# A diffusion mixer layer with two kinds of heads: the recurrence stage's PE work put in the order of the text

## The chip, the core and the metric

The kernel runs on one core of a Trainium2 chip. The metric is the device time of one execution in microseconds, the median of several runs. A profiled execution gives the trace; its span is the time from its first to its last instruction.

The engines are TensorE (PE, with its weight loads as PEld), VectorE (DVE), ScalarE (ACT), GpSimd (POOL) and SyncE (SP), which issues most DMAs.

## The reference

One layer on 1024 latent and 256 context tokens of width 1024, all in float32: a modulated RMSNorm, one input projection, a differential-attention group (8 heads), a bidirectional RWKV-7 recurrence (16 heads of 64 in two directions), an output projection over both, a gated residual and a final RMSNorm.

```python
h = rmsnorm(x, norm_g) * (1 + scale) + shift
q, k, v, g_a, u_b, g_b = split(h @ w_in)
# attention, per head: two score maps, their softmaxes p
a = p[:, :, 0] - lam * p[:, :, 1]
o_a = rmsnorm(einsum('bhqk,bkhv->bqhv', a, v), subln_g) * (1 - lam_init) * silu(g_a)
# recurrence, per head and direction (reversed for d = 1)
def step(S, (r_t, w_t, k_t, v_t, kk_t, b_t)):
    sa = einsum('bhvk,bhk->bhv', S, -kk_t)
    S = S * w_t + sa * b_t + v_t * k_t
    return S, einsum('bhvk,bhk->bhv', S, r_t)
y = y_forward + y_backward
o_b = (groupnorm(y) * lnx_g + lnx_b + bonus) * silu(g_b)
out = rmsnorm(x + gate * (concat(o_a, o_b) @ w_out), final_g)
```

Latent tokens also attend to 512 cached context tokens, and their scans start from a cached state; the layer returns the keys, the values and the final states of the context too.

## The kernel before

**Stages.** Up to 1243 us the kernel projects the tokens and writes the operands of the recurrence to scratch in DRAM. Then `mix_phase` runs the recurrence, and beside it the attention and most of the output projection. What is left of these and the final norm is the tail, from 2392 us on.

**The recurrence in chunks.** A scan is cut into chunks of 32 tokens, so that a step handles a whole chunk by matrix products. A step handles four pairs of heads (`NL`), both heads of a pair and both directions. The four pairs are two *duos* `w`, each with a bank of PSUM, `bank[w]`. There are 80 steps: two groups of pairs, five segments of 256 tokens (the context and four latent ones), eight chunks each. Two steps (`HN`) form a *part* `j`, whose operands lie in the slot `slots[w, j % 2]`: `L` (the weights) and `R` (the moving side, with the state in rows 0 to 63, the values in 64 to 95, and sa in 96 to 127). The two slots of a duo take turns.

**One step**, `step(j, k, fill)`, is in the text:
1. the *sa* group, L894: 8 products of 96 rows for each bank, each f32 product being two instructions in the profile; ACT copies the result to `R[96:128]` (L899, four copies for each bank);
2. `fill(0)`, a portion of attention and other background work;
3. the *st* group, L908, 8 products for each bank; DVE multiplies the result by the decay into the state of the next step (L917, two operations for each bank);
4. `fill(1)`, a second portion;
5. the *y* group, L931, 8 products for each bank, into another part of the same bank; ACT copies it to `ys` (L933).

sa and st are put ahead by `high_priority(offset=500)` (`HPC`), y isn't (`HPY = 0`). The order on each engine isn't that of the text: a scheduler sets it, by priorities and by its estimate of when operands are ready, so it may cut a group in two and put attention between.

**Slots.** At the first step of part j, `load_part(j + 1)` fills the other slot, last read by the y groups of part j − 1. For each duo these are one load of `kt` into `L` (L772), two of `ra` into `L` (L775) and four of `vb` into `R` (L781); `load_inv` adds one of a chunk's inverse, `Tb`, for each duo (L792, three buffers, `TBUF`). Ahead of the second step of part j, `prep(j + 1, w)` multiplies `Tb` with rows of `L` for each duo (L802, all into one bank `yb`) and ACT copies that back to `L` (L805). SP issues these loads in its own order, and each waits there for the slot.

**Attention** is a generator. For a block n of 128 queries of a head: `scores(n, m, c)` (L1047) makes one 512-key chunk of map m, DVE takes it out of PSUM with a maximum (L1050) and ACT the exponential (L1058); `combine` (L1078, DVE) subtracts the second map; `trans` (L1086) turns a chunk on PE in four products and ACT copies it to `aT` (L1088); `values` (L1101) multiplies four pieces of it with the values. Each yield tells a cost, and `fill` takes as many pieces as its credit allows; the credit grows in each step by the whole cost over the number of steps, times `RATE`, 0.86. `turn` also advances `outs` (the norm of attention's result; `ob` at L1138 on POOL), `norms` (the norm of y, which reads `y` from DRAM into `yn`) and `projs`.

**Projection.** `project(j)` does a quarter of the output projection (the rows of two attention heads and two pairs) for ten token tiles, each of eight products in three forms (L1286 to L1288, into PSUM `pso`), and adds to `acc` in DRAM (L1280). The fourth quarter is done in the tail by `final`, which also applies the gate (L1357) and adds the residual (L1358, both on POOL).

## Time and profile before

| what | us |
|---|---|
| runs: 2642.70, 2634.27, 2647.06; median | 2642.7 |
| the profiled execution | 2639.98 |
| its span | 2637.7 |
| projection, to | 1243 |
| recurrence, 80 steps, to | 2392 |
| tail, to | 2638 |

The busy share of each engine, the causes of PE's waits and the granted clock stand in the prediction, with the rows themselves. In a row of instructions stand the line, the engine and the operation, then what is written and what is read, how many, and busy time and mean ns of one. The part behind the second bar is the time for which the engine stood idle just before these instructions, and whose end it was that ended it. In a row of the timeline stand the start, the time until the end of the last of the instructions put together, and what they are. The column PEclk is the clock granted to TensorE as a share of full speed.

The DMA queues, as the page has them, move these transfers of the recurrence:

```profile
L<-kt SPq DMA_DIRECT2D x80, 512.0 KB
L<-ra SPq DMA_DIRECT2D x160, 128.0 KB
R<-vb SPq DMA_DIRECT2D x320, 32.0 KB
y<-ys SPq DMA_DIRECT2D x160, 64.0 KB
yn<-y SPq DMA_DIRECT2D x20, 512.0 KB
```

### The profile page before, as it was taken

The numbers are of one execution on the slowest core, as the hardware profiler recorded it, in microseconds if no ns is written. First come the engines' busy times: TensorE is split into PE (matmuls) and PEld (weight loads), VectorE is DVE, ScalarE is ACT, GpSimd is POOL, SyncE is SP. The second block draws the span as 40 slices with busy tenths as digits, with TensorE's granted clock in tenths as the row PEclk, the third lists the DMA queues.
The fourth block names the chain that finished last, engine by engine and source line by source line (L and its number), as shares of the span: only waits on it lengthen the run. The fifth ranks groups of instructions, "written<-read, shape, count | busy, mean of one in ns | idle before, by whom it ended". The sixth has DMA issues, their size and how long they took to land. (4 is left out here: it accounts for less than half of the span.)

```text
span 2637.7 us, 61554 instructions
## 1 busy us (share of the span) xinstructions
PE 2361.2 (90%) x23907; PEld 1908.8 (72%) x23907; DVE 1475.6 (56%) x2960; ACT 1274.8 (48%) x2928; POOL 1199.6 (45%) x1735
## 2 busy tenths in 40 slices
PE   6999999999999999998688888888889898898886
PEld 4788888888888888786466766666666676676664
DVE  5656565555455655434457556664455455566466
ACT  3334443333333433322476666766556357674243
POOL 4234344243433443375365525747467542125386
PEclk9999999999999999998798889889989999999997
DMA  7465656565645565567878777878867887676534
GB/s 237 111 165 131 177 147 176 135 169 161 160 129 155 136 176 131 167 158 185 176 155 187 162 160 145 184 164 191 211 155 194 203 198 171 141 171 220 176 104 161
DMA packets 532418, 437.63 MB, mean 166 GB/s; under 512 B 161991, under 2 KB 466291, under 8 KB 532128
## 3 DMA queue, kind: packets, MB, share of 16 engines
q1 hardware_dynamic: 530032, 427.96, 64.9%
q0 software_dynamic: 2096, 5.75, 1.1%
q8 instruction: 188, 3.08, 0.5%
q14 instruction: 102, 0.84, 0.1%
HBM read 258.69 MB, written 163.86 MB: 160 GB/s over the span
## 5 line engine op out<-in xcount | busy, mean ns | idle before, releaser
L1047 PE MATMUL sc<-ka,q 128*128 128x512 f32 (+1 forms) x832 | 296.7, 457 | 20.2 <-DVE pb L1050 12.3
L1050 DVE TENSOR_SCALAR_CACHE_REDUCE pb<-sc,mn 128x512 f32<-128x512 f32 x256 | 191.7, 749 | 135.1 <-PE sc L1047 110.4
L1101 PE MATMUL po<-vk,aT 128*128 128x128 f32 x1600 | 244.8, 296 | 9.1 <-ACT aT L1088 8.6
L1058 ACT ACTIVATE pb<-pb,mn 128x1536 f32<-128x1536 f32 (+1 forms) x160 | 218.4, 1366 | 60.2 <-DVE pb L1050 58.7
L1101 PEld LDWEIGHTS po<-vk,aT 128*128 128x128 f32 x1600 | 221.3, 205 | 29.4 <-ACT aT L1088 12.2
L479 POOL TENSOR_SCALAR ta<-ta,ka 128x256 f32<-128x256 f32 x80 | 88.1, 1101 | 297.8 <-DVE bk L477 297.7
L734 POOL TENSOR_TENSOR tmp<-aw,tt 128x31 f32<-128x31 f32 (+15 forms) x310 | 164.6, 531 | 127.9 <-DMA aw<-kt 54.9
L456 ACT COPY km<-ptk 64x256 f32<-64x256 f32 x320 | 117.4, 367 | 192.1 <-PE ptk L453 165.7
L899 ACT COPY R<-bank 32x128 f32<-32x128 f32 x640 | 163.4, 255 | 68.7 <-PE bank L894 59.4
L917 DVE TENSOR_TENSOR R<-bank,wc 64x256 f32<-64x256 f32 x312 | 131.4, 421 | 113.5 <-PE bank L908 98.4
L736 POOL TENSOR_TENSOR tt<-tt,tmp 128x31 f32<-128x31 f32 (+15 forms) x310 | 182.4, 588 | 18.2
L1047 PEld LDWEIGHTS sc<-ka,q 128*128 128x128 f32 x832 | 145.6, 208 | 55.7 <-DVE pb L1050 21.5
L1078 DVE SCALAR_TENSOR_TENSOR pb<-pb,cc,pb 128x512 f32<-128x512 f32 (+1 forms) x208 | 170.6, 866 | 2.5
L805 ACT COPY L<-yb 32x384 f32<-32x384 f32 x312 | 146.3, 469 | 40.1 <-PE yb L802 35.9
L802 PE MATMUL yb<-L,Tb 32*32 32x96 f32 x2496 | 96.1, 261 | 76.3 <-DMA L<-kt 68.7
L450 DVE TENSOR_TENSOR km<-pg,msk 128x512 f32<-128x512 f32 x80 | 55.1, 689 | 183.5 <-PE pg L449 168.7
L1050 DVE TENSOR_SCALAR_CACHE_REDUCE pb<-sc 128x512 f32<-128x512 f32 (+1 forms) x160 | 101.2, 635 | 91.2 <-PE sc L1047 75.3
L1088 ACT COPY aT<-pa 128x512 f32<-128x512 f32 (+1 forms) x208 | 115.9, 570 | 62.9 <-PE pa L1086 60.5
L1086 PE MATMUL pa<-ident,pb 128*128 128x128 f32 x800 | 133.2, 292 | 14.0 <-ACT acc L1278 7.8
L802 PEld LDWEIGHTS yb<-L,Tb 32*32 32x32 f32 x2496 | 62.6, 111 | 105.9 <-DMA L<-kt 56.3
L908 PEld LDWEIGHTS bank<-R,L 128*64 128x64 f32 x2560 | 99.3, 151 | 54.6 <-ACT R L899 23.7
L908 PE MATMUL bank<-R,L 128*64 128x64 f32 x2560 | 122.9, 243 | 16.7 <-ACT R L899 16.4
(355 smaller groups left out, 6463.2 us busy)
## 6 DMA issues: line engine op xcount, KB each, us to landing
kt<-km SPq DMA_DIRECT2D x160, 256.0 KB
L<-kt SPq DMA_DIRECT2D x80, 512.0 KB
acc<-acc SPq DMA_DIRECT2D x50, 512.0 KB
ra<-ra SPq DMA_DIRECT2D x160, 128.0 KB
L<-ra SPq DMA_DIRECT2D x160, 128.0 KB
R<-vb SPq DMA_DIRECT2D x320, 32.0 KB
y<-ys SPq DMA_DIRECT2D x160, 64.0 KB
yn<-y SPq DMA_DIRECT2D x20, 512.0 KB
```

The lines of the kernel that those rows point to most:

```text
L734: e.tensor_tensor(mv, aw[:n, t, t + 1:CH].unsqueeze(2).broadcast_to([n, w, j]), tt[:n, t:t + 1, 0:j].broadcast_to([n, w, j]), op=ALU.mult)
L736: e.tensor_tensor(tt[:n, t + 1:CH, 0:j], tt[:n, t + 1:CH, 0:j], mv, op=ALU.add)
L802: nc.tensor.matmul(pp[32 * q:32 * q + 32, n:n + 96], Tb[96:128, e, HN * q + c, :], L[96:128, e, q // 2, q % 2, c, 0:96], start=True, stop= ...
L805: nc.scalar.copy(L[96:128, :, q // 2, q % 2, :, 0:96], pp[32 * q:32 * q + 32, 0:192 * HN].rearrange("p (e c y) -> p e c y", e=2, y=96))
L899: nc.scalar.copy(R[96:128, k, e, :, hv(h)], bank[w][u:u + 32, 0:128].rearrange("p (d v) -> p d v", d=2))
L908: nc.tensor.matmul(bank[w][hv(h), o_:o_ + 64], L[:, e, h, d, k, 0:64], R[:, k, e, d, hv(h)], start=True, stop=True, tile_position=(0, 64 * h))
L1047: nc.tensor.matmul(sc, q[:, v, m, qc], ka[:, m, 0:kn], start=(v == 0), stop=(v == 1))
L1050: nc.vector.tensor_scalar(pm[:, c * 512:c * 512 + kn], sc, -0.125, mn[:, c - 1:c] if c else None, op0=ALU.mult, op1=ALU.min, accum_out=mn[ ...
L1058: nc.scalar.activation(v, v, AF.Exp, bias=mn[:, c:c + 1], scale=-1.0, accum_out=B["l3"][:, m, k:k + 1])
L1078: nc.vector.scalar_tensor_tensor(a, B["p"][1][:, v], B["cc"], a, op0=ALU.mult, op1=ALU.add)
L1086: nc.tensor.transpose(pt[:, t * P:(t + 1) * P], B["p"][0][:, 512 * c + t * P:512 * c + (t + 1) * P], ident)
L1101: nc.tensor.matmul(po, B["aT"][c][:, t * P:(t + 1) * P], vk[:, t, :], start=(c == 0 and t == 0), stop=(c == last and t == nt - 1))
```

## The change

1. **PE in the order of the text.** Just ahead of `att = attention()` the kernel enters `tc.manual_schedule(engines={nc.tensor.engine})`. From there to the end PE's instructions stand as the text has them; the scheduler still orders the other engines.
2. **The step in the text.** sa for both banks; the copies to `R[96:128]`, those of the second bank now on DVE; at the second step of a part `prep` of the first duo; `fill(0)`; st for both banks; the state update; y for both banks directly behind it; `prep` of the second duo; `fill(1)`. `R` and the bank hold direction ahead of pair now. The priority stays around the copies and the state update.
3. **Attention's pieces** come in another order: scores of the first map alternate with `values` of the block before the last, scores of the second map with `trans` of the last block, and `combine` is done at the end of its own block. `aT` has three buffers for two; a copy per block (`l3` to `l`) goes. `fill`'s rate is 1.06 in the first half of the steps and 0.68 in the second.
4. **Slots in fewer transfers.** `kt` and `ra` lie in scratch by pairs of pairs, so that a duo's `ra` is one load; `vb` comes in two loads for each duo and `Tb` in one for both duos (one buffer). Nine loads a part take the place of 16, both `kt` first, `Tb` third in the text. `y` is stored in 4 transfers for 8, of runs of 1 KB for 512 bytes, and read back by two loads for one.
5. **Projection.** The quarters of the second group of pairs are started after segment 0 instead of 3, so that two tiles of the third quarter come in the recurrence and not in the tail, and the residual add moves from POOL to DVE. Yields are added: `NDEL` and `ODEL` grow from 6 and 8 to 10 and 14, and `project` and `final` get two more each.

On PE, in the middle of the first part of the recurrence, a step looked as follows before; L894 is the sa group (of `bank1` here), L802 the build, L908 st, L931 y, and the rows with `sc`, `pa` and `po` are scores, `trans` and `values` of attention.

```order
L894 MATMUL bank1_12299<-R11_11594,L11_11593 32x64 x8
L802 MATMUL yb_12300<-L00_11563,Tb0_2_12714 32x96 x9
L908 MATMUL bank0_12298<-R01_11574,L01_11573 64x64 x8
L1047 MATMUL sc0_1_1_1_12496<-ka_0_1_12312,q_0_0_12304 128x512 x2
L802 MATMUL yb_12300<-L00_11563,Tb0_2_12714 32x96 x7
L1086 MATMUL pa0_0_0_12483<-ident_78,pb0_12301 128x128 x4
L1086 MATMUL pa0_0_1_12592<-ident_78,pb0_12301 128x128 x4
L908 MATMUL bank1_12299<-R11_11594,L11_11593 64x64 x8
L1047 MATMUL sc0_1_1_2_12587<-ka_0_2_12315,q_0_0_12304 128x512 x2
L931 MATMUL bank0_12298<-R01_11574,L01_11573 32x64 x8
L1047 MATMUL sc0_2_0_0_12651<-ka_0_0_12309,q_0_0_12304 128x512 x2
L1101 MATMUL po0_0_12603<-vk_0_0_12318,aT0_0_0_12488 128x128 x4
```

And a like step after the change, where L893 is sa, L803 the build, L913 st, L936 y, and L1057, L1089 and L1104 are scores, `trans` and `values`.

```order
L893 MATMUL bank0_12282<-R01_11574,L01_11573 32x64 x8
L893 MATMUL bank1_12283<-R11_11594,L11_11593 32x64 x8
L803 MATMUL yb_12284<-L00_11563,Tb2_12707 32x96 x16
L1057 MATMUL sc0_3_1_1_12902<-ka_0_1_12298,q_0_0_12290 128x512 x2
L1089 MATMUL pa0_2_2_12906<-ident_78,pb0_12287 128x128 x4
L1057 MATMUL sc0_3_1_2_12913<-ka_0_2_12301,q_0_0_12290 128x512 x2
L1104 MATMUL po0_2_12927<-vk_0_0_12304,aT0_2_0_12841 128x128 x4
L1057 MATMUL sc0_4_0_0_12937<-ka_0_0_12295,q_0_1_12324 128x512 x2
L1104 MATMUL po0_2_12927<-vk_0_1_12306,aT0_2_1_12852 128x128 x4
L913 MATMUL bank0_12282<-R01_11574,L01_11573 64x64 x8
L913 MATMUL bank1_12283<-R11_11594,L11_11593 64x64 x8
L936 MATMUL bank0_12282<-R01_11574,L01_11573 32x64 x8
```

Before, the two st groups stood apart, with scores and transposes between, and the y group of `bank0` came two rows behind the second of them, that of `bank1` 18 rows behind (not shown); now both banks of a group stand side by side, and y behind st with nothing between (the row of y of `bank1` is the next). Here the y group waits for DVE's state update, which reads the same bank. From the first row of the recurrence on PE to its last, the kind of work (attention and projection, sa, st, y, build, transposes of the state) changed 1013 times from row to row before, and changes 478 times now. The products of that stretch are nearly the same: 746 scores and 742 now, 700 `trans` and 700 `values` in both, and 160 and 176 of each of the projection's three forms.

On SP's queue, the loads of one part's slots looked as follows before (`L00` and `L10` are `L` of the two duos).

```order
L772 DMA L00_11563<-kt_67 64x2x1024
L775 DMA L00_11563<-ra_66 64x8x64 x2
L781 DMA R00_11564<-vb_68 32x2x128 x4
L772 DMA L10_11583<-kt_67 64x2x1024
L775 DMA L10_11583<-ra_66 64x8x64 x2
L781 DMA R10_11584<-vb_68 32x2x128 x4
L792 DMA Tb1_2_12716<-td0_77 32x2x256
```

And so they look now.

```order
L781 DMA R00_11564<-vb_68 32x2x256
L772 DMA L00_11563<-kt_67 64x2048
L772 DMA L10_11583<-kt_67 64x2048
L793 DMA Tb2_12707<-td0_77 32x4x256
L781 DMA R00_11564<-vb_68 32x2x256
L782 DMA L00_11563<-ra_66 64x16x64
L781 DMA R10_11584<-vb_68 32x2x256 x2
L782 DMA L10_11583<-ra_66 64x16x64
```

The two `kt` loads stood apart by six transfers and now follow each other; `Tb` came last and now stands behind them.

The diff, cut:

```diff
@@ -42,12 +42,12 @@
-RATE = 0.86
+RATES = (1.06, 0.68)
...
-TBUF = 3
+TBUF = 1
...
-NDEL = 6
-ODEL = 8
+NDEL = 10
+ODEL = 14
...
@@ -769,16 +769,18 @@
-            nc.sync.dma_start(L[64:128].rearrange("r e h d c y -> r e (h d c y)"),
-                              s["kt"][p:p + 2, sg + 1, f].rearrange("e r h d y -> r e (h d y)"))
-            for e in range(2):
-                nc.sync.dma_start(L[0:64, e, :, :, :, 64:128].rearrange("r h d c y -> r (h d c) y"),
-                                  s["ra"][p + e, sg + 1, f].rearrange("r h d (c y) -> r (h d c) y", y=HD))
+            nc.sync.dma_start(L[64:128].rearrange("r e h d c y -> r (e h d c y)"),
+                              s["kt"][p // 2, sg + 1, f].rearrange("r e h d y -> r (e h d y)"))
+        load_inv(j)
+        for w in duos:
+            p = p0 + 2 * w
+            L, R = slots[w, j % 2]
...
-                for c in range(HN):
-                    t1 = t0 + CH * (HN - 1 - c if d else c)
-                    nc.sync.dma_start(R[64:96, c, :, d, :], s["vb"][t1:t1 + CH, p * P:(p + 2) * P].rearrange("t (e v) -> t e v", e=2))
+                src = s["vb"][t0:t0 + CH * HN, p * P:(p + 2) * P].rearrange("(c t) y -> t c y", t=CH)
+                nc.sync.dma_start(R[64:96, :, d].rearrange("t c e v -> t c (e v)"), src[:, ::-1] if d else src)
+            nc.sync.dma_start(L[0:64, :, :, :, :, 64:128].rearrange("r e h d c y -> r e (h d c) y"),
+                              s["ra"][p // 2, sg + 1, f].rearrange("r e h d (c y) -> r (e h d c) y", y=HD))
...
@@ -884,53 +884,62 @@
-        with ahead(HPC):
-            for w in duos:
-                L, R = slots[w, j % 2]
-                for d in range(2):
-                    for e in range(2):
-                        for h in range(2):
-                            u = 64 * e + 32 * h
-                            nc.tensor.matmul(bank[w][u:u + 32, 64 * d:64 * d + 64], L[0:96, e, h, d, k, 96:128],
-                                             R[0:96, k, e, d, hv(h)], start=True, stop=True, tile_position=(0, u))
+        for w in duos:
+            L, R = slots[w, j % 2]
+            for d in range(2):
...
-                        nc.scalar.copy(R[96:128, k, e, :, hv(h)], bank[w][u:u + 32, 0:128].rearrange("p (d v) -> p d v", d=2))
-        fill(0)
+                        nc.tensor.matmul(bank[w][u:u + 32, 64 * d:64 * d + 64], L[0:96, e, h, d, k, 96:128],
+                                         R[0:96, k, d, e, hv(h)], start=True, stop=True, tile_position=(0, u))
...
-                L, R = slots[w, j % 2]
+                R = slots[w, j % 2][1]
...
-                    for d in range(2):
-                        for h in range(2):
-                            o_ = 256 + 128 * e + 64 * d
-                            nc.tensor.matmul(bank[w][hv(h), o_:o_ + 64], L[:, e, h, d, k, 0:64],
-                                             R[:, k, e, d, hv(h)], start=True, stop=True, tile_position=(0, 64 * h))
+                    for h in range(2):
+                        u = 64 * e + 32 * h
+                        (nc.vector.tensor_copy if w else nc.scalar.copy)(
+                            R[96:128, k, :, e, hv(h)], bank[w][u:u + 32, 0:128].rearrange("p (d v) -> p d v", d=2))
+        later_prep = k == HN - 1 and j + 1 < n_part
+        if later_prep:
+            prep(j + 1, 0, yb)
+        fill(0)
+        for w in duos:
+            L, R = slots[w, j % 2]
+            for e in range(2):
+                for d in range(2):
+                    for h in range(2):
+                        o_ = 256 + 128 * d + 64 * e
+                        nc.tensor.matmul(bank[w][hv(h), o_:o_ + 64], L[:, e, h, d, k, 0:64],
+                                         R[:, k, d, e, hv(h)], start=True, stop=True, tile_position=(0, 64 * h))
+        with ahead(HPC):
+            for w in duos:
...
-                    dst = R[0:64, k + 1]
+                    dst = slots[w, j % 2][1][0:64, k + 1]
...
-                    nc.vector.tensor_tensor(dst[:, :, :, hv(h)], bank[w][hv(h), 256:512].rearrange("p (e d v) -> p e d v", e=2, d=2),
-                                            wcs[p0][hv(h), 2 * w:2 * w + 2, sg + 1, :, c:c + 1].broadcast_to([HD, 2, 2, HD]), op=ALU.mult)
-        fill(1)
+                    nc.vector.tensor_tensor(dst[:, :, :, hv(h)], bank[w][hv(h), 256:512].rearrange("p (d e v) -> p d e v", e=2, d=2),
+                                            wcs[p0][hv(h), 2 * w:2 * w + 2, sg + 1, :, c:c + 1].rearrange("p e d o -> p d e o").broadcast_to([HD, 2, 2, HD]), op=ALU.mult)
...
-        with ahead(HPY):
-            for w in duos:
-                L, R = slots[w, j % 2]
-                for e in range(2):
-                    o_ = P + 64 * e
-                    for h in range(2):
-                        for d in range(2):
-                            q = 64 * d + 32 * h
-                            nc.tensor.matmul(bank[w][q:q + 32, o_:o_ + 64], L[:, e, h, d, k, 64:96], R[:, k, e, d, hv(h)],
-                                             start=True, stop=True, tile_position=(0, q))
-                nc.scalar.copy(ysb[m, g][:, c % 4, 2 * w:2 * w + 2], bank[w][:, P:2 * P].rearrange("p (e v) -> p e v", e=2))
+        for w in duos:
+            L, R = slots[w, j % 2]
+            for e in range(2):
+                o_ = P + 64 * e
+                for h in range(2):
+                    for d in range(2):
+                        q = 64 * d + 32 * h
+                        nc.tensor.matmul(bank[w][q:q + 32, o_:o_ + 64], L[:, e, h, d, k, 64:96], R[:, k, d, e, hv(h)],
+                                         start=True, stop=True, tile_position=(0, q))
+        for w in duos:
+            nc.scalar.copy(ysb[m, g][:, c % 4, 2 * w:2 * w + 2], bank[w][:, P:2 * P].rearrange("p (e v) -> p e v", e=2))
+        if later_prep:
+            prep(j + 1, 1, yb)
+        fill(1)
...
@@ -1191,25 +1194,37 @@
...
-            if p is not None:
-                weight(p)
-                combine(p, 0)
-            if pp is not None:
-                values(pp, len(st[pp]["ch"]) - 1)
+                if c < nk - 1 and vp:
+                    old_values()
+                    yield 0.87
+            while vp:
+                old_values()
...
-            if p is not None:
-                trans(p, 0)
-                yield 0.43
-            for c in range(nk):
-                if c < kp_ - 1:
-                    combine(p, c + 1)
-                scores(n, 1, c)
-                yield cost
-            for c in range(nk, kp_ - 1):
-                combine(p, c + 1)
+            for c in range(max(nk, kp_)):
+                if c < kp_:
+                    trans(p, c)
+                    yield 0.43
+                if c < nk:
+                    scores(n, 1, c)
+                    yield cost
+            if new:
+                weight(n)
+                for c in range(nk):
+                    combine(n, c)
+            if kp_ > 1:
+                values(p, 0)
+                yield 0.87
...
@@ -1355,7 +1369,7 @@
-                nc.gpsimd.tensor_tensor(x, x, y, op=ALU.add)
+                nc.vector.tensor_tensor(x, x, y, op=ALU.add)
...
@@ -1371,6 +1385,7 @@
+    ctx.enter_context(tc.manual_schedule(engines={nc.tensor.engine}))
...
@@ -1384,14 +1399,13 @@
-    rate = total / (2 * n_tick) * RATE
...
-            state["credit"] += rate / 2
+            state["credit"] += total / (4 * n_tick) * RATES[2 * state["t"] // n_tick]
...
@@ -1422,10 +1436,6 @@
-                load_inv(j + 1)
-        if k == HN - 1 and j + 1 < n_part:
-            for w in duos:
-                prep(j + 1, w, yb)
...
@@ -1436,7 +1446,7 @@
-        if sg == 3:
+        if sg == (3 if m < 5 else 0):
...
```

71 lines of the change are left out of this document (34 added, 37 removed).

## The prediction

> **What bounds the kernel now.** The first view is the busy time by engine.
>
> ```profile
> PE 2361.2 (90%) x23907; PEld 1908.8 (72%) x23907; DVE 1475.6 (56%) x2960; ACT 1274.8 (48%) x2928; POOL 1199.6 (45%) x1735
> ```
>
> PE is the engine nearest to full, and the change alters its order from the recurrence on. The second view cuts the rest of the span at the first recurrence matmul (1243 us), in the middle of the 80 steps (1800) and at their end (2392).
>
> ```profile
> core 0: us, PE busy (x) PEld busy (x) DVE busy (x) ACT busy (x) POOL busy (x), PEclk, DMA share, GB/s
> 1243.00:1800.00 557.00, 463.55 (x6905) 358.62 (x6905) 335.67 (x832) 367.91 (x953) 296.99 (x545) 0.87 0.79 167
> 1800.00:2392.00 592.00, 524.12 (x6747) 400.72 (x6750) 316.74 (x773) 361.83 (x927) 263.37 (x451) 0.93 0.78 184
> 2392.00:2638.00 246.00, 192.24 (x958) 152.09 (x946) 149.28 (x302) 84.01 (x176) 139.17 (x157) 0.89 0.48 163
> ```
>
> In the recurrence PE stands still for 557 − 463.6 + 592 − 524.1 = 161 us of 1149 (14.4 us a step in the mean), and works at 0.87 and 0.93 of its clock. DVE is busy for 0.60 and 0.54 of it, so it isn't the bound there yet. The third view says what ended PE's idle time between 1243 and 2392 us.
>
> ```profile
> engine line waited for: us in total, times, longest us
> PE yb L802 <- DMA L<-kt: 68.7, 31, 10.1
> PE bank L908 <- ACT R L899: 16.4, 16, 3.3
> PE bank L894 <- ACT ys L933: 13.0, 10, 2.7
> PE sc L1047 <- DVE pb L1050: 9.1, 9, 4.1
> PE pso L1286 <- DVE acc L1280: 8.5, 2, 8.2
> PE pa L1086 <- ACT acc L1278: 7.8, 2, 5.9
> PE po L1101 <- ACT aT L1088: 7.8, 8, 3.1
> ```
>
> One wait stands out: L802, which builds the operands of the next two steps, waits 31 times for the kt load of its slot. The next largest is four times smaller. The last lines that matter here are the groups of the instructions that the change moves, in the same stretch: PE first, then DVE.
>
> ```profile
> L802 PE MATMUL yb<-L,Tb 32*32 32x96 f32 x2496 | 96.1, 261 | 76.3 <-DMA L<-kt 68.7 <-ACT pb L1058 2.7 <-ACT L L805 2.3
> L931 PE MATMUL bank<-R,L 128*32 128x64 f32 x2540 | 82.1, 235 | 4.5 <-DVE R L917 4.5
> ```
>
> ```profile
> L917 DVE TENSOR_TENSOR R<-bank,wc 64x256 f32<-64x256 f32 x312 | 131.4, 421 | 113.5 <-PE bank L908 98.4 <-DMA wc<-wc 5.6 <-ACT aT L1088 3.6
> L1078 DVE SCALAR_TENSOR_TENSOR pb<-pb,cc,pb 128x512 f32<-128x512 f32 (+1 forms) x182 | 147.0, 853 | 2.1
> L1050 DVE TENSOR_SCALAR_CACHE_REDUCE pb<-sc,mn 128x512 f32<-128x512 f32 x228 | 170.7, 749 | 125.8 <-PE sc L1047 104.9 <-PE pa L1086 12.9 <-DVE pb L1050 0.5
> ```
>
> The y group L931 waits for the state update L917 for 4.5 us in all 80 steps. That small number is the weight of this case: the change puts the y group directly behind the st group, so that this wait is met in every step.
>
> **Slot loads: −65 us.** The wait as it looks in the timeline:
>
> ```profile
> 1604.37 0.59 SPq L772 DMA_DIRECT2D L<-kt  x1
> 1605.75 0.69 PE L908 MATMUL bank<-R,L 128*64 128x64 f32 x16
> 1606.40 0.74 DVE L1050 TENSOR_SCALAR_CACHE_REDUCE pb<-sc,mn 128x512 f32<-128x512 f32 x1
> 1607.68 0.85 DVE L917 TENSOR_TENSOR R<-bank,wc 64x256 f32<-64x256 f32 x2
> 1610.80 0.85 PE L802 MATMUL yb<-L,Tb 32*32 32x96 f32 x28 [2.51 <-DMA L<-kt]
> 1611.58 0.43 PE L931 MATMUL bank<-R,L 128*32 128x64 f32 x16
> 1612.59 0.59 SPq L772 DMA_DIRECT2D L<-kt  x1
> ```
>
> A slot may be refilled only after the y group of its last step has read it, and y stands at the very end of the step, behind both portions of attention, and slides further as the last choice of the order. The kt load of one duo is issued at 1604.4, and that of the other at 1612.6, right behind the y group of the other bank (1611.58 + 0.43): 8.2 us later. L802 gets the first one 6.4 us after its issue. Afterwards both y groups stand together and ahead of the second portion of attention, both kt loads stand next to each other on SP's queue, and between that y and the build stand half a step, a whole one and the next sa, some 20 us at 14.4 a step, for a load of 6.4; the mean wait was 68.7/31 = 2.2 us, the longest 10.1. I take 65 of the 76.3 us of L802 away and leave 11 for the longest ones. Bounds: −76 and 0 (release not earlier, or the longer transfers land later). PE then waits next for the y group itself, below.
>
> **Fewer changes of kind on PE: −30 us.** Between the first and last recurrence matmul the order of PE changes between kinds of work 1013 times before and 478 times afterwards, 535 fewer. The price of one, from two like transposes:
>
> ```profile
> 1707.22 0.60 PE L1086 MATMUL pa<-ident,pb 128*128 128x128 f32 x4
> 1707.66 1.06 PE L1101 MATMUL po<-vk,aT 128*128 128x128 f32 x8
> 1708.55 0.60 PE L1086 MATMUL pa<-ident,pb 128*128 128x128 f32 x4
> 1709.08 0.69 PE L908 MATMUL bank<-R,L 128*64 128x64 f32 x16
> 1709.69 0.43 PE L931 MATMUL bank<-R,L 128*32 128x64 f32 x16
> 1710.06 0.73 PE L1047 MATMUL sc<-ka,q 128*128 128x512 f32 x2
> ```
>
> Four transposes followed by another full-array product take 0.44 us from start to start, and followed by a recurrence group 0.53: 0.09 us for the way in. The way back shows nothing (y to scores 0.37, less than its 0.43). So 535 × 0.09 = 48 if every change costs it, 24 if only one of two does. I take 30; bounds −10 and −55.
>
> **Waits of st for the copies of R and of sa for ys: −25 us.** Of 16.4 + 13.0 = 29.4 us most goes, since a whole portion of attention now stands between sa and st, and the ys copy has the second portion to run beside. Half of the R copies moves from ACT to DVE (4 a step), which can bring new waits there. Bounds −29 and +20.
>
> **The y group behind the state update: +86 us.** From the rows above: at 1605.75 the st group of a bank takes 0.69, ends at 1606.44, and the update ends at 1608.53, 2.1 us later, since two evictions of L1050 were ahead on DVE. Undisturbed, the update starts about 0.1 us behind its group and both halves take 2 × 0.42. Now all four updates (4 × 0.421 = 1.68) follow two st groups, and the two y groups stand on PE right behind, with nothing between. From the end of bank 0's st group: the updates end at 0.11 + 1.68 = 1.8, y can start its second bank some 0.15 later, and in that time PE has 0.69 (st of bank 1) + 0.43 (y of bank 0) to do: 1.95 − 1.12 = 0.8 us of standing, at least, in each step. At most, one combine (0.853) and one eviction (0.749) are ahead on DVE: 0.8 + 1.6 = 2.4. DVE is busy with other things for about half of the time, with operations of some 0.75 us, so the mean addition is near 0.5 × 0.75 = 0.4 or, since recurrence work goes first, less: I take 0.3, so 1.1 us, nearer to the floor. 78 steps with an update: 78 × 1.1 = 86; bounds 62 and 187. Behind the waiting y rows on PE stand the building of the second duo's operands and the second portion of attention; DVE's evictions and ACT's exponentials starve with them.
>
> **The start of attention: +10 us.**
>
> ```profile
> 1243.70:1258.90 15.20, 9.14 (x208) 6.65 (x208) 3.31 (x9) 8.20 (x26) 6.10 (x11) 0.64 0.86 225
> 1265.17 1.19 PE L1047 MATMUL sc<-ka,q 128*128 128x512 f32 x2 [6.30 <-DMA ka<-klo]
> ```
>
> The first keys land at 1265.2. Before, PE does 9.1 us of recurrence work meanwhile; now the first scores stand in the text behind the first sa group, and everything behind them waits. I take +10; bounds 0 and +20.
>
> **The clock: −10 us.** The windows of 3.4 us around the wait above:
>
> ```profile
> 1606.30:1609.70 3.40, 1.99 (x32) 1.40 (x26) 2.97 (x9) 2.47 (x6) 3.09 (x5) 1.00 0.98 192
> 1609.70:1613.10 3.40, 2.30 (x52) 1.75 (x52) 0.10 (x1) 2.28 (x6) 2.93 (x7) 1.00 0.03 8
> 1613.10:1616.50 3.40, 3.40 (x40) 2.65 (x38) 2.50 (x7) 2.83 (x5) 2.96 (x6) 0.50 0.90 199
> ```
>
> Two windows with PE busy for 1.99 and 2.30 of 3.40 us are followed by one at half clock. At a granted clock of 0.87 and 0.93 the recurrence loses 557 × 0.13 + 592 × 0.07 = 114 us of PE's full-speed time. The long slot waits go, but a stand of about 1.1 us is added to each step, which alone leaves 2.3 of 3.4 us busy, the share of the second row. So I credit 10 of the 114; bounds −100 and +40. The Trainium skill, page "TensorE: Matmul & The Clock Gate", section "Why this matters for your kernels", says it otherwise: only idle gaps of more than about 3 us between bursts bring the clock down. The rows here disagree, as the longest gap in the two windows is the 2.51 us before L802; by that page of the Trainium skill the new short stands would cost no clock, which is the first rival below.
>
> **The tail: −12 us.**
>
> ```profile
> PE pxo L1144 <- POOL ob L1138: 11.2, 3, 9.5
> L1286 PE MATMUL pso<-wohi,ohi 128*128 128x512 f32 x80 | 34.3, 429 | 9.4 <-ACT ohi L1270 5.5 <-DVE acc L1280 2.7 <-DVE bv L996 0.8
> L1358 POOL TENSOR_TENSOR x<-x,y 128x1024 f32<-128x1024 f32 x10 | 24.9, 2487 | 3.3 <-DMA x<-x_sample 2.6 <-DMA x<-x_prompt 0.7
> L1280 DVE TENSOR_TENSOR acc<-pso,acc 128x512 f32<-128x512 f32 x20 | 13.3, 688 | 36.9 <-PE pso L1288 17.7 <-DMA acc<-acc 16.0 <-PE pso L1287 3.1
> ```
>
> Two of ten tiles of a projection move from the tail into the recurrence, 16 × 3 matmuls of 0.43 = 20.6 us of PE, which is no gain by itself where PE is the bound in both. The residual add costs 2.49 us on POOL and by the half-size row of DVE about 2 × 0.69 = 1.4: about 1 us for each of the last two on the end chain. Seven tiles instead of one stand behind the last attention and can cover the 9.5 us wait for POOL's ob: −9.5 − 2, about −12. Against it, the final product's weights are loaded with only about 5 us of PE work beside them. Bounds −30 and +25.
>
> **Everything else at nothing.** In text order a row that isn't ready holds all rows behind it. The four attention and projection waits in the table (9.1 + 8.5 + 7.8 + 7.8 = 33) may go, as attention is spread with more distance, or grow to half a microsecond in each step (+40). I take 0. The rates 1.06 and 0.68 move attention to the first half and remove none of it; the y stores and norm loads run on queues that no PE wait of the table names.
>
> **The sum.** The profiled execution took 2639.98 us, its span 2637.7. −65 − 30 − 25 + 86 + 10 − 10 − 12 = −46: 2640 − 46 = **2594 us**. The median of the runs shown is 2642.7, 2.7 above this execution.
>
> **Rivals.**
> - *The clock stays up.* If the gate wants a longer gap than 1.1 us, the stands cost only themselves, and with the slot waits gone about half of the 114 us comes back instead of 10: −50 more, 2544 us. For it: the longest waits (10.1) are the slots'. Against it: the rows at 1606 and 1609. The section of the Trainium skill named above has this rule.
> - *Even.* The stand of y costs 1.1 + 46/78 = 1.7 us a step and takes everything back: 2640.
> - *Slower: y behind a full DVE.* From 1.7 us a step on, the kernel gets slower. DVE gets 4 copies of R a step (half of L917's 0.42 for half as many elements a row, an estimate: 0.8 us of 14.4) and, by the rates, 1.06/0.86 = 1.23 of the attention in the first half, where attention is about two thirds of its work: 335.7/557 = 0.60 busy becomes 0.60 × 1.15 + 0.06 = 0.75, in bursts of three combines (2.6 us) at a block's end. If the update waits behind such a burst, the price is 2.4 us: 2594 + 78 × 1.3 = 2695. Against it: L917 comes first in the order of DVE wherever it is ready, and for a mean of 1.7 more than half of the steps, (1.7 − 0.8)/1.6, would have to meet the top price.
> - *The loads are no earlier.* If kt still lands late, the 65 us stay: 2659. Against it: nothing stands between the two loads any more.
>
> **Chances.** Forecast 0.48, clock 0.17, even 0.12, full DVE 0.18, loads 0.05. What a measurement of this kernel can tell from no change is about 0.5%, 13 us. Faster: 0.17 and nearly all of the forecast's 0.48, 0.62. Same: 0.12 and 0.04 from the edges of the forecast and of the loads' case, 0.16. Slower: 0.18 and 0.04 of the loads' case, 0.22. The range, 2500 to 2690, takes in the clock's case and most of the slower one, with the bounds of the y term (−24, +101) and of the clock term; the forecast's own is 2550 to 2630.
>
> **What would show it.** L802's wait for kt falls under 15 us; the y line waits for DVE's state update in nearly every step, 60 to 110 us in total with a mean near 1.1 over two banks; waits of st for ACT's copies shrink; the first half's granted clock stays between 0.85 and 0.92; the span from the first to the last step falls from 1149 to about 1110 us. Wrong would be: a y wait of over 130 us, a clock near 1.0, or L802 still waiting.

## The result and the profile after

The change makes the kernel slower: 2736.15 us (median of 4 runs) beside 2638.48 us, a ratio of 1.037 with an interval of 1.0346 to 1.0393. The prediction was 2594 us, faster by 46. The profiled execution has a span of 2738.4 us, 100.7 more than before. Cut at the first sa row and the end of the last y row of the timeline, the stages are:

| stage | before, us | after, us |
|---|---|---|
| up to the recurrence | 1243 | 1250 |
| recurrence | 1152 | 1239 |
| tail | 243 | 249 |

The 7 us up to the recurrence lie within what that stage varies by: it takes 1238 to 1250 us in the profiled executions of all kernels here.

The busy time of the new execution, and its windows, with the recurrence cut in its 40th step:

```profile
PE 2308.9 (84%) x23907; PEld 1899.5 (69%) x23907; DVE 1564.8 (57%) x3210; ACT 1202.9 (44%) x2606; POOL 1181.5 (43%) x1725
```

```profile
core 0: us, PE busy (x) PEld busy (x) DVE busy (x) ACT busy (x) POOL busy (x), PEclk, DMA share, GB/s
1250.00:1887.00 637.00, 459.54 (x6920) 370.91 (x6908) 400.88 (x1011) 350.87 (x823) 390.40 (x718) 0.87 0.77 153
1887.00:2489.00 602.00, 483.35 (x6796) 387.34 (x6796) 337.72 (x840) 309.42 (x739) 171.45 (x268) 0.89 0.74 175
```

PE is busy for 52 us less with the same 23907 instructions, so the longer time is all standing: 637 − 459.5 + 602 − 483.4 = 296 us in the recurrence, where it was 161. The waits of PE in this stretch say where:

```profile
engine line waited for: us in total, times, longest us
PE bank L936 <- DVE R L924: 168.0, 154, 29.9
PE sc L1057 <- DVE pb L1060: 35.1, 22, 9.1
PE sc L1057 <- DMA ka<-klo: 24.1, 3, 21.9
PE pa L1089 <- ACT aT L1091: 11.9, 10, 2.6
```

```profile
L803 PE MATMUL yb<-L,Tb 32*32 32x96 f32 x2496 | 73.5, 258 | 4.5 <-DMA Tb<-td 4.3 <-ACT L L806 0.2
```

The slot wait is gone (76.3 us before, 4.5 now), and in its place stands the wait of the y group for the state update: 154 waits in 78 steps, two a step, 168 us where it was 4.5. A quiet step, with PE and DVE together (L1292 is the projection's addition, L924 the update of both banks):

```profile
2251.00 1.15 PE L913 MATMUL bank<-R,L 128*64 128x64 f32 x32
2251.11 0.69 DVE L1292 TENSOR_TENSOR acc<-pso,acc 128x512 f32<-128x512 f32 x1 [3.35 <-PE pso L1300]
2251.81 1.74 DVE L924 TENSOR_TENSOR R<-bank,wc 64x256 f32<-64x256 f32 x4
2252.72 0.43 PE L936 MATMUL bank<-R,L 128*32 128x64 f32 x16 [0.56 <-DVE R L924]
2253.60 0.43 PE L936 MATMUL bank<-R,L 128*32 128x64 f32 x16 [0.46 <-DVE R L924]
```

y of the first bank waits 0.56 us and y of the second 0.46, although the update began right behind the first bank's st: DVE needs 1.74 us for its four operations, and PE has only the groups themselves to do. That is the floor, 1.0 us in this step and in more than half of all steps (the median of the 80 is 1.02). The longest single wait is something else:

```profile
1749.06 0.69 DVE L1060 TENSOR_SCALAR_CACHE_REDUCE pb<-sc 128x512 f32<-128x512 f32 x1 [0.53 <-PE sc L1057]
...
1778.35 0.69 DVE L983 TENSOR_REDUCE m<-yn 128x8 f32<-128x512 f32 x1 [28.59 <-POOL yn L980]
1778.95 0.15 DVE L1074 RECIPROCAL cc<-l 128x1 f32<-128x1 f32 x1
1779.07 0.76 DVE L984 TENSOR_SCALAR m<-m 128x8 f32<-128x8 f32 x1
1779.74 0.36 DVE L1075 SCALAR_TENSOR_TENSOR cc<-cc,l,neglam 128x1 f32<-128x1 f32 x1
1780.03 0.85 DVE L924 TENSOR_TENSOR R<-bank,wc 64x256 f32<-64x256 f32 x2
```

DVE stands for 28.6 us with the norm's reduction at the head of its queue. That waits for POOL's addition of `yn`, whose load is late:

```profile
1751.91 4.86 SPq L726 DMA_DIRECT2D aw<-kt  x5
...
1771.43 1.88 SPq L971 DMA_DIRECT2D yn<-y  x3
```

```profile
1777.05 1.26 POOL L980 TENSOR_TENSOR yn<-yn 128x512 f32<-128x512 f32 x1
```

SP was issuing other loads and stores until then. POOL itself had stood for 21.8 us with L734 at the head of its queue, for the loads of `aw`, until 1776.14. The state update, whose operands had been ready since 1751, stood behind the reduction, PE's y group behind the update, and everything else of PE behind y:

```profile
1749.84 1.15 PE L913 MATMUL bank<-R,L 128*64 128x64 f32 x32
1780.93 0.65 PE L936 MATMUL bank<-R,L 128*32 128x64 f32 x16 [29.94 <-DVE R L924]
```

Added up over all the stands of y by what DVE did in them: 85 us are the updates themselves, 28 combines (L1081) ahead of them, 29 the reduction L983 waiting, about 8 the reciprocal L1074 waiting (7 of it for ACT's exponentials), 7 evictions (L1060), and the rest small. So about half is the floor and half is DVE's queue.

### The profile page after: what moved, and what is told of

The parts are those of the page before. It is cut to its first block, busy times and chain, and to the rows that moved or that the text cites. A ratio compares the mean times of both kernels' runs of the same rounds, so it can differ in the third digit from the quotient of the medians.

```text
span 2738.4 us, 60831 instructions
## 1 busy us (share of the span) xinstructions
PE 2308.9 (84%) x23907; PEld 1899.5 (69%) x23907; DVE 1564.8 (57%) x3210; ACT 1202.9 (44%) x2606; POOL 1181.5 (43%) x1725
## 3 DMA queue, kind: packets, MB, share of 16 engines
q1 hardware_dynamic: 514352, 427.94, 63.6%
## 4 chain that ended last, share of the span: by engine, by line
PE 47%; DMA 17%; DVE 14%; POOL 7%; ACT 7%; SPq 5%; issue 4%; DVEq 0%; POOLq 0%; ACTq 0%
PE sc L1057 4%; PE po L1104 4%; DVE R L924 4%; PE pg L449 2%; PE pa L1089 2%; DVE pb L1081 2%; ACT pb L1068 2%; PE pso L1298 2%; PE pso L1300 2%; PE pso L1299 2%; PE yb L803 2%; DVE pb L1060 2%; ACT L L806 1%; DMA acc<-acc 1%; PE ptk L453 1%
## 5 line engine op out<-in xcount | busy, mean ns | idle before, releaser
L1057 PE MATMUL sc<-ka,q 128*128 128x512 f32 (+1 forms) x832 | 313.0, 467 | 61.4 <-DVE pb L1060 36.8
L1060 DVE TENSOR_SCALAR_CACHE_REDUCE pb<-sc,mn 128x512 f32<-128x512 f32 x256 | 191.9, 750 | 145.1 <-PE sc L1057 137.2
L1104 PEld LDWEIGHTS po<-vk,aT 128*128 128x128 f32 x1600 | 224.9, 207 | 24.0 <-ACT aT L1091 6.2
L1104 PE MATMUL po<-vk,aT 128*128 128x128 f32 x1600 | 233.0, 293 | 4.1 <-ACT aT L1091 4.1
L734 POOL TENSOR_TENSOR tmp<-aw,tt 128x31 f32<-128x31 f32 (+15 forms) x310 | 164.2, 530 | 157.3 <-DMA aw<-kt 55.5
L936 PE MATMUL bank<-R,L 128*32 128x64 f32 x2560 | 74.1, 239 | 168.2 <-DVE R L924 168.0
L1057 PEld LDWEIGHTS sc<-ka,q 128*128 128x128 f32 x832 | 142.8, 211 | 93.4 <-DVE pb L1060 53.4
L936 PEld LDWEIGHTS bank<-R,L 128*32 128x32 f32 x2560 | 46.5, 116 | 192.7 <-DVE R L924 192.5
L1089 PE MATMUL pa<-ident,pb 128*128 128x128 f32 x800 | 139.6, 301 | 43.8 <-DVE pb L1081 15.8
L1081 DVE SCALAR_TENSOR_TENSOR pb<-pb,cc,pb 128x512 f32<-128x512 f32 (+1 forms) x208 | 170.3, 868 | 2.5
L1089 PEld LDWEIGHTS pa<-ident,pb 128*128 128x128 f32 x800 | 105.2, 154 | 79.5 <-issue 21.8
L1060 DVE TENSOR_SCALAR_CACHE_REDUCE pb<-sc 128x512 f32<-128x512 f32 (+1 forms) x160 | 101.7, 637 | 87.4 <-PE sc L1057 84.4
L924 DVE TENSOR_TENSOR R<-bank,wc 64x256 f32<-64x256 f32 x312 | 131.2, 421 | 31.5 <-PE bank L913 23.1
L1282 POOL TENSOR_TENSOR olo<-of,ohi 128x512 fp32r<-128x512 f32 x30 | 40.3, 1344 | 214.2 <-ACT ohi L1281 200.9
L939 ACT COPY ys<-bank 128x128 f32<-128x128 f32 x160 | 41.5, 265 | 199.3 <-PE bank L936 183.7
```

The lines of the kernel that those rows point to most:

```text
L734: e.tensor_tensor(mv, aw[:n, t, t + 1:CH].unsqueeze(2).broadcast_to([n, w, j]), tt[:n, t:t + 1, 0:j].broadcast_to([n, w, j]), op=ALU.mult)
L924: nc.vector.tensor_tensor(dst[:, :, :, hv(h)], bank[w][hv(h), 256:512].rearrange("p (d e v) -> p d e v", e=2, d=2), wcs[p0][hv(h), 2 * w:2 ...
L936: nc.tensor.matmul(bank[w][q:q + 32, o_:o_ + 64], L[:, e, h, d, k, 64:96], R[:, k, d, e, hv(h)], start=True, stop=True, tile_position=(0, q))
L1057: nc.tensor.matmul(sc, q[:, v, m, qc], ka[:, m, 0:kn], start=(v == 0), stop=(v == 1))
L1060: nc.vector.tensor_scalar(pm[:, c * 512:c * 512 + kn], sc, -0.125, mn[:, c - 1:c] if c else None, op0=ALU.mult, op1=ALU.min, accum_out=mn[ ...
L1081: nc.vector.scalar_tensor_tensor(a, B["p"][1][:, v], B["cc"], a, op0=ALU.mult, op1=ALU.add)
```

## The experiments

**Theory 1:** the y group next to st puts every delay of DVE on PE. **Theory 2:** it is the fixed order as such, which holds PE at whichever row is late. **Theory 3** concerns the prediction's gains, whether the slots' loads, y's place or the order removed the slot wait. Each ratio below is to runs of the kernel before on the same chip.

| run | median us | ratio, interval | recurrence | tail |
|---|---|---|---|---|
| the change | 2736.15 | 1.037, 1.0346 to 1.0393 | 1239 | 249 |
| e1 y at the end | 2666.44 | 1.012, 1.0089 to 1.0151 | 1184 | 235 |
| e2 combine in the next block | 2736.42 | 1.037, 1.0333 to 1.0406 | 1246 | 252 |
| e3 ordered by the scheduler | 2616.05 | 0.992, 0.989 to 0.9951 | 1149 | 227 |
| e4 before, with slots' loads | 2624.65 | 0.9968, 0.9938 to 0.9998 | 1153 | 249 |
| e5 y in the middle | 2612.75 | 0.9883, 0.985 to 0.9915 | 1120 | 247 |
| e6 norm later | 2724.69 | 1.0309, 1.0272 to 1.0346 | 1185 | 300 |
| e7 start later | 2711.12 | 1.0258, 1.0214 to 1.0301 | 1196 | 261 |
| e8 e5, e6 and e7 | 2648.59 | 1.0008, 0.9986 to 1.003 | 1084 | 320 |
| e9 e8, norm's delay moved | 2660.4 | 1.0083, 1.0053 to 1.0113 | 1156 | 261 |
| e10 e5 and e7 | 2634.26 | 0.9988, 0.9964 to 1.0012 | 1138 | 257 |
| e11 e2, DVE in text order | 2810.15 | 1.0661, 1.0632 to 1.069 | 1291 | 275 |
| e12 e9 with e11's two edits | 2832.33 | 1.0746, 1.0712 to 1.0781 | 1250 | 339 |
| e13 e5, order fixed in recurrence | 2589.03 | 0.9817, 0.9783 to 0.985 | 1107 | 227 |
| e14 before, with tail's parts | 2641.87 | 1.0012, 0.9988 to 1.0037 | 1157 | 228 |
| e15 one piece between st and y | 2647.3 | 1.0039, 1.0012 to 1.0066 | 1156 | 245 |
| e16 e5, copies on ACT | 2617.2 | 0.9933, 0.9902 to 0.9965 | 1120 | 249 |

The last two columns are microseconds of each one's profiled execution, cut as above. That execution lies 25 us above the median in e4, 17 below it in e14, 13 below in e13 and at most 6 from it in the others. The runs were made on several chips, on which the kernel before had medians from 2635.27 to 2647.81; a difference between two rows of the table is therefore better read from their ratios (1 point is 26 us) than from their medians.

### y's place: e1, e5 and e15

e1 moves the y group behind `fill(1)`, where it stood in the text before (the diffs show the main lines, with `...` for what is left out, against the changed kernel where nothing else is said):

```diff
+        if later_prep:
+            prep(j + 1, 1, yb)
+        fill(1)
         for w in duos:
             L, R = slots[w, j % 2]
...
-        if later_prep:
-            prep(j + 1, 1, yb)
-        fill(1)
```

> The changed kernel with only the y group moved behind the second portion of attention, as its place in the text was before. Theory 1 (PE stands because y is next to the state update, so that every delay of DVE's queue reaches PE): of the 168 us that y waits, the floor of about 0.95 us in each of 78 steps (74 us) goes, and most of the stands of up to 6 us, since some 5 us of attention stand between; the 33 us of step 32 stay in part. About 2625 us, 95 to 125 us faster than the change. Theory 2 (a fixed order holds PE at whatever row is late): the waits move to scores and sa, and the gain is below 40 us, 2700 or more.

70 us less than the change (2.5 points), less than theory 1 wanted. Its waits show why:

```profile
PE bank L893 <- ACT ys L942: 88.2, 79, 13.2
PE sc L1057 <- DVE pb L1060: 49.4, 38, 11.0
```

The wait of y is gone from the top of the list, but the next step's sa now stands behind y in the same way, and waits in 79 steps for ACT to read y out of the bank. The same neighbourhood, one group further. So e5 puts y between the two halves of the portion, with attention on both sides:

```diff
+        if later_prep:
+            prep(j + 1, 1, yb)
+        fill(1, 0)
         for w in duos:
             L, R = slots[w, j % 2]
...
-        if later_prep:
-            prep(j + 1, 1, yb)
-        fill(1)
+        fill(1, 1)
...
-    def fill(pos):
-        for _ in range(2):
+    def fill(pos, part=None):
+        for _ in range(2 if part is None else 1):
...
```

> The changed kernel with the y group in the middle of the second portion of attention: attention stands between st and y, and between y and the next step's sa, and the order stays fixed. Theory 1 (what costs is that a PE group stands next to the one whose result another engine must first read out of the same bank, y behind the state update, sa behind the copy of ys): both the 0.95 us a step of the change and the 88 us that sa waited with y at the end go; 2590 to 2620, and what is left of waiting is at scores and transposes, for DVE. Theory 2 (a fixed order waits somewhere anyway): the wait moves to a third row, 2660 or more.

2612.75 us, 123 below the change (4.9 points) and 1.2% faster than before, with the order still fixed. Both waits shrink:

```profile
PE bank L893 <- ACT ys L942: 19.4, 11, 6.1
PE bank L939 <- DVE R L924: 15.9, 22, 2.6
```

e15 asks how much distance is needed. It leaves all in its place and takes one piece of attention between st and y:

```diff
+        piece()
         for w in duos:
             L, R = slots[w, j % 2]
             for e in range(2):
                 o_ = P + 64 * e
...
```

> The changed kernel with one piece of attention (0.4 to 1 us of PE) between the st group and the y group, all else in its place. If the neighbourhood is the cost, and the updates themselves are its floor (0.95 us a step): y's wait falls from 168 to 80 to 110 us and the time by 50 to 80 us, to 2655 to 2690. If only long distances help, since DVE's combines and late loads make the wait: y's wait stays above 130 and the time above 2705.

It gains 89 us over the change (3.3 points). The step at the same place as the quiet one above, with one chunk of scores (L1058) between:

```profile
2252.09 1.15 PE L913 MATMUL bank<-R,L 128*64 128x64 f32 x32
2252.19 0.69 DVE L1293 TENSOR_TENSOR acc<-pso,acc 128x512 f32<-128x512 f32 x1 [2.66 <-PE pso L1301]
2252.89 1.74 DVE L924 TENSOR_TENSOR R<-bank,wc 64x256 f32<-64x256 f32 x4
2253.17 0.73 PE L1058 MATMUL sc<-ka,q 128*128 128x512 f32 x2
2253.83 0.43 PE L937 MATMUL bank<-R,L 128*32 128x64 f32 x16
...
2254.69 0.43 PE L937 MATMUL bank<-R,L 128*32 128x64 f32 x16 [0.42 <-DVE R L924]
```

```profile
PE bank L937 <- DVE R L924: 69.2, 93, 5.2
```

The scores fill the first of the two stands, and the second stays. y waits 69 us in 93 stands instead of 168 in 154. Of the 99 us between them up to 25 are the single stand of 29.9 us, which one piece can't cover and which doesn't occur here: the longest is 5.2, and DVE's longest stand at the norm's reduction is 10.2. The rest, over 70 us, is the piece's own. Theory 1 holds: 0.4 to 1 us of work at the right place is worth more than half of the whole effect. No run puts y into a bank of its own, so whether the wait would go without any distance isn't known.

### The order itself: e3

e3 leaves out the one line that fixes PE's order.

```diff
-    ctx.enter_context(tc.manual_schedule(engines={nc.tensor.engine}))
```

> The changed kernel without the line that fixes PE's order: the scheduler orders PE again, by the new text and with no priority for the matmuls. Theory 2 (the fixed order is what costs): near or below the kernel before, 2640 or less. Theory 1 (the neighbourhood of y and the state update, and DVE's queue): the scheduler can put attention between st and y, so some of the floor goes, but DVE's queue still stands for late loads and exponentials; 2660 to 2700.

2616.05 us, 0.8% faster than before and nearly as fast as e5. This alone would fit theory 2; e5 tells them apart, since there the order is fixed and the loss is gone too. The two differ in how: the scheduler puts attention between st and y (y waits 8.1 us), but PE's busy time rises to 2358.8 us, at a granted clock of 0.945 for the change's 0.927, and the slot wait comes back:

```profile
PE yb L803 <- DMA L<-kt: 48.6, 20, 7.8
PE yb L803 <- DMA y<-ys: 20.6, 3, 11.2
```

### The slots: e4

e4 is the kernel before with the layouts of part 4 (`kt`, `ra`, `vb`, `Tb`, `y`, and `R` with direction ahead of pair) and nothing else; the diff is to the kernel before, and is that of the loads shown with the change.

> The kernel before with only the new layout and the fewer transfers of slots, y and its reading (R with direction ahead of pair, TBUF 1). If the loads were the part that gives (the prediction's 65 us for slot loads rests on them and on y's place): 20 to 40 us faster than before with L802's wait for kt halved. If the release by y decides alone: within 10 us of before, the wait still above 60 us. If the new transfers are themselves late: slower than before by over 13 us.

12 us below before by the medians, with an interval that just leaves out 1; the wait for `kt`, in an execution 25 us above the median, is the old one:

```profile
PE yb L803 <- DMA L<-kt: 73.3, 30, 10.2
```

Fewer transfers don't shorten this wait. From the end of a slot's last y group to the start of the next build from it there are 4.3 us before (median over the parts), 5.5 here and 7.1 in e3, but 19.7 with the change, 15.4 in e5, and 14.1 in e1, where y stands at the very end of its step in the text and the slot wait is 2.2 us nonetheless. So neither the loads nor y's place in the text is what removes the wait, but PE's fixed order: without it the scheduler builds early and does y late.

### What stands ahead in DVE's queue: e2, e6, e11 and e12

e2 does `weight(p)` and `combine(p)` a block later, behind the first scores of the next block.

> The changed kernel with weight and combine of a block done one block later, behind the first scores of the next block, where the exponentials are long done. Theory 1: the 45 us that DVE stands at the reciprocal for ACT's exponential, in front of the state update, go; the floor of y stays. 25 to 45 us faster than the change, about 2700. Theory 2: no place of a DVE operation matters much, within 10 us of the change.

No difference, and no test: only PE's order is fixed by the text, and from the recurrence on DVE's operations stand in the trace in the same order as with the change (DVE's stand at L1074 is 42.5 us, 44.7 with the change). e11 therefore fixes DVE's order to the text too.

```diff
+    ctx.enter_context(tc.manual_schedule(engines={nc.tensor.engine, nc.vector.engine}))
```

> The changed kernel with weight and combine one block later, and with DVE's order fixed to the text too, so that the edit reaches DVE's queue (with the scheduler ordering DVE it kept its place there). y still stands next to the update. If the reciprocal's stand for the exponential (42 to 46 us on DVE) reaches PE through the state update: y's wait falls from 164 to about 120 and the time to 2690 to 2710. If combines (2.5 us) now stand ahead of the update in the text's order, they take its place: 2730 or more, with y's wait above 160.

74 us slower than the change; y waits 169.2 us. The reduction's long stand is gone from this wait, and the combines in it have grown from 28 to 49 us, so the second line of the expectation came true. It doesn't explain the 74 us, since y waits no longer than with the change (168.0). PE, whose instructions stand in the same order as with the change, is busy for 2370.2 us instead of 2308.9, at a granted clock of 0.905 for 0.927, and the tail is 26 us longer; why this is so stays open. e12 adds the same two edits to e9 (below).

> The edits of the first of these four, with combine one block later and DVE in the text's order. If the waits of scores and transposes for DVE (about 50 us with y in the middle) come from DVE standing at reciprocals and reductions: below the first of these four by 10 to 30 us. If the scheduler's order of DVE is the better one, slower than it.

It is the slowest of all: the scheduler's order of DVE is the better one. y waits only 53.6 us here; what PE waits for most are the norm's values from POOL (L1005 for `yn`), 159.1 us where it was 18.3 in e9. e6 treats the other stand and uses the norm's load three steps later.

```diff
-        yield
-        yield
+        for _ in range(14):
+            yield
         m = pool.tile([P, 2, 4], F32, tag="m", name=f"m{nm}", bufs=2)
```

> The changed kernel with 12 more yields in norm between the load of y and its first use, about three steps. The theory: the state update stands in DVE's queue behind the norm's reduction, which waits for POOL's add and that for the load (65 us, one of 29). Then these stands go and y's longest waits with them: 40 to 55 us faster than the change, y's wait near 125. Rival: the long stands come from PE's own lateness, and DVE's queue only shows them: within 10 us of the change.

The recurrence is 54 us shorter, and y's longest wait falls from 29.9 to 10.3. But the gain isn't the expected one: y's total stays at 161.7, where 125 was expected, as the floor, the combines and some stands at the reduction remain. Norms that end later hold up the projection's tiles, which then fall out of the recurrence: 384 of its products run there instead of 528, 46 us less of PE, and the tail is 51 us longer. What is left is 11 us by the medians and 0.6 points by the ratios, near the rival's line.

### The start: e7, e8, e9 and e10

e7 begins attention with a debt of two steps.

```diff
+    state["credit"] = -2 * total / n_tick
```

> The changed kernel whose attention gets no credit for the first two steps, so that the first scores stand behind them in PE's order, and not behind the first sa. The 24 us that the first scores wait for keys and queries fall to under 10, as 2 steps of recurrence are done meanwhile: 10 to 16 us faster than the change. If those two steps are held up elsewhere (attention then lacks at the end), no gain.

The wait for the first keys falls from 24.1 to 7.0 us, and the time by 25; the longest y wait is 5.4 here, so the 30 us stand didn't occur, and the two can't be told apart in this run. e8 puts y in the middle with e6 and e7:

> All three edits together: y in the middle of the second portion, the norm's use later, attention's start later. If the three causes add: about 2540 to 2570, below both kernels. If the norm's stand costs nothing once y doesn't hang on the state update: no faster than y in the middle with the later start, 2575 to 2605.

The shortest recurrence of all, 1084 us, and a tail of 320: as in e6, only 384 of the projection's products run in the recurrence. e9 tries to keep the one without the other, with `NDEL = 0`:

> As the three edits together, but the norm's delay is moved and not added: 12 more yields between load and use, NDEL 0 instead of 10 at its end. If the 73 us by which the tail grew with the three edits came from norms that end later, so that the projection's tiles fall out of the recurrence: the recurrence stays near 1084 us, the tail returns to about 250, and the time is 2575 to 2595. If the tail grew for attention's missing two steps: the tail stays near 320, 2640 or more.

The tail returns to 261, but the recurrence, which has its 528 products again, to 1156: no gain. For a good part the 1084 us were work put off to the tail. e10 leaves the norm as it was:

> y in the middle of the second portion and attention's start two steps later, the norm as in the change. If the start's 24 us wait is the cost and is covered by two steps of recurrence: 2588 to 2600, 13 to 25 us below y in the middle alone. If the credit that attention lacks comes back in the tail: 2605 to 2620.

21 us above e5 by the medians, 1 point by the ratios. The 15 us saved at the first keys are gone by step 20, which both reach 298 us after their first, and the rest is lost behind it. Which piece of attention then stands beside which group has changed for the whole stage. Whether that is the reason, and why it costs so much, stays open.

### The tail, and the best version: e13, e14 and e16

e13 is e5 with the fixed order ended in front of the tail.

```diff
-    ctx.enter_context(tc.manual_schedule(engines={nc.tensor.engine}))
+    fixed = ctx.enter_context(ExitStack())
+    fixed.enter_context(tc.manual_schedule(engines={nc.tensor.engine}))
...
+    fixed.close()
     close_recurrence()
```

> y in the middle of the second portion, and PE's order fixed in the recurrence alone: the scheduler orders the tail. If the fixed order costs the tail its 20 us (247 against 227 with the scheduler): 2590 to 2600, below every run so far. If the tail's length comes from what the recurrence leaves over: within 6 us of y in the middle, 2607 to 2619.

2589.03 us, the fastest run: 1.8% below the kernel before, and 0.7 points better than e5. The tail has 227 us, as in e3, for 247; where the order of the tail is fixed it has 235 us (e1) or more.

> The kernel before with only the second group's projection started after segment 0 and the residual add on DVE. The prediction's term for the tail was -12 us: 2620 to 2632, with the wait of 9.5 us for POOL's ob gone. If the moved tiles only lengthen the recurrence by what the tail loses: within 6 us of before.

e14, the kernel before with the earlier projection and the add on DVE alone, is no faster than before: its tail is 15 us shorter and its recurrence 5 longer in the one profile, which is of its fastest execution, and the medians show nothing beyond their interval. e16 is e5 with the copies of the second bank's sa back on ACT.

> y in the middle of the second portion with the copies of the second bank's sa back on ACT. DVE loses 93 us of work in the recurrence, ACT gains about 80. If the scores' and transposes' waits for DVE (37 + 25 us) come from DVE's load: 10 to 25 us faster than with the copies on DVE, 2588 to 2603. If st then waits for ACT's copies as before (16 us in the kernel before): equal or slower, 2610 to 2635.

e16 is no faster than e5, and half a point slower by the ratios: DVE is busy for 92 us less, and the waits of PE's scores and transposes for it fall by 8 us (from 62.1 to 53.8). st waits for ACT's copies for 3.8 us only. With y in the middle, moving these copies back gains nothing.

## Why the prediction was wrong, step by step

- **y behind the update, +86: the step that failed, by its size.** It measured 168.0 − 4.5 = 163.5 us, 2.1 a step, near the upper bound of 187. The floor was reckoned at 0.8 and is about 1.0; the updates alone make 85 us, which was the whole term. What I added for DVE's queue, 0.3 us a step, took the mean of random operations in flight and assumed that recurrence work goes first on DVE. The trace shows otherwise: combines come three at a time (28 us in all), and the update, ready since 1751, stood for 28.6 us behind a reduction that itself waited for a late load. An operation's own length, which is all that the term counted, doesn't hold the time that it stands waiting at the head of the queue. The sign that the prediction named for being wrong, a y wait of over 130 us, came.
- **Everything else at nothing.** The scores' wait for DVE grew from 9.1 to 35.1 us, so the cover that I named, attention spread with more distance, wasn't there for them; the other three waits of that term went from 24 to some 14 us.
- **Slot loads, −65.** 72 us went: right in size. The distance was right too, 19.7 us for the "some 20" between y and the build. The reason was wrong: I credited y's place and the loads' order, and e4, e3 and e1 show that it is the order of PE.
- **Fewer changes of kind, −30.** PE's busy time fell by 52 us over the span, with no fewer instructions, and e3 shows most of that coming back (2358.8, at a better clock) when the scheduler interleaves again. Larger than I took, near the upper bound of 55, although the busy time holds the clock's part as well: e11, with the change's order of PE, has 2370.2 at a lower clock.
- **Waits of st and sa for copies, −25.** 29.4 us before, some 9 now. Right.
- **The start, +10.** The wait for the first keys grew by 17 us. Right in kind, small in size.
- **The clock, −10.** It got worse, 0.88 in the mean of the recurrence for 0.90: of the windows of 3.4 us, 87 of 365 in the recurrence have a clock below 0.75, where it was 68 of 339. These three rows of the change tell how:

```profile
1443.80:1447.20 3.40, 3.40 (x77) 2.60 (x77) 3.08 (x10) 2.31 (x8) 0.00 (x0) 1.00 0.53 119
1447.20:1450.60 3.40, 1.18 (x8) 0.65 (x6) 1.50 (x5) 3.33 (x7) 1.48 (x8) 1.00 0.38 80
1450.60:1454.00 3.40, 3.19 (x13) 3.00 (x14) 1.24 (x3) 1.23 (x3) 3.01 (x7) 0.51 0.25 60
```

A single thin window is followed by one at half speed; PE's only stand in it, from 1448.4 to 1450.8, is 2.43 us long. The section "Why this matters for your kernels" of the Trainium skill's page "TensorE: Matmul & The Clock Gate" wants a gap of about 3 us for that; there was none here. So the first rival, the clock that stays up, fell.

- **The tail, −12.** It grew by 6 us. e14 and e13 show why: moving tiles is worth nothing in all, and the fixed order costs the tail 20 us. I hadn't reckoned with an order of text that isn't spaced there. The 48 products that moved are also worth less than the 20.6 us that I gave them, since they overlap on PE: with them gone the projection's products take 56.1 us of PE in the tail for 63.6.
- **The rivals.** The slower case had the right mechanism and the right point (from 1.7 us a step on), at a chance of 0.18. With 2.15 us a step it would have given 2594 + 78 × 1.05 = 2676. Of the 60 us that are left, the scores' waits (26), the tail (18), the start (7) and the stage ahead of the recurrence (7) make 58, but other waits grew by some 20 and the busy time gained more than I took, so this is a sum and not a proof. The clock's part in it isn't shown by any run.

## What to carry to other kernels

When an order is fixed by hand, each row waits for what the engine before it has yet to do: before a group is put directly behind another whose result a second engine must read, put at least that engine's own time of other work between them, on both sides of the group. To price such a wait, add to that engine's own time what can stand ahead in its queue, operations that come in bursts and operations that themselves wait for a load above all; the mean length times the busy share misses both. And look at the order of every engine that isn't fixed: an edit of the text that doesn't reach its queue tests nothing.

## What the runs showed of the hardware

PE's clock fell to 0.51 after a window of 3.4 us with 1.18 us of work and no gap of 3 us in it. Of 41 falls of the clock in the recurrence of the change, 32 had less than 3 us without work at a time in the 10 us ahead. And the same 23907 PE instructions were busy for 2361.2, 2308.9, 2287.6 and 2268.2 us in four orders (before, the change, e5, e13): how work is interleaved on PE, with the clock that follows, was worth 93 us with no instruction removed. The order of PE alone isn't all of it: in e11, where PE's order is that of the change and only DVE's differs, they were busy for 2370.2 us at a granted clock of 0.905.
